# Norm steps fed tile by tile and a pinned matmul order between the dense blocks of a 1024-wide network

## The chip, the cores and the metric

The kernel runs on one core of a Trainium2 chip. The metric is the device time of one execution in microseconds, the median of several executions. The core has five engines that each run their own instruction queue in order: PE (matrix multiply), DVE and POOL (element-wise), ACT (functions, scaled copies) and SP, which issues the loads and stores.

## The reference

The program is two blocks on 512 tokens of width 1024, all in fp32. The first block has two layers: a mixer, a layer norm, a convolutional feed-forward network (FFN), a second layer norm, and an embedding gate. The second block has two hybrid layers with an RMS norm ahead of each, and a final RMS norm. What matters here:

```
for i in range(DEPTH):                                     # 2
    y = mixer_ab(x, ...) if i % 2 == 0 else mixer_c(x, ...)
    x = layer_norm(ALPHA * x + y, ln_mix_g[i], ln_mix_b[i])
    f = conv_ffn(x, ...)                                   # 1024 -> 2816 -> 1024
    x = layer_norm(ALPHA * x + f, ln_ffn_g[i], ln_ffn_b[i])
    x = x + sigmoid(x @ ple_w_gate[i]) * (p[i] @ ple_w_proj[i])
for l in range(DEPTH):
    x = hybrid_layer(x, norm_g[l], w_in[l], ...)           # begins with rmsnorm(x, norm_g)
return rmsnorm(x, final_norm_g)
```

## The kernel before

Activations lie feature-major: `s.x` is eight tiles of 128 features x 512 tokens. Every fp32 matmul is done as three in a reduced fp32 format, from a high and a low part of both operands: `mm3` (lines 351 to 353). The parts come from `split`: ACT rounds to the high part (L400), DVE subtracts to get the low part (L401). Weights arrive as 512 KB units by SP's queue and are split the same way (L326 on ACT, L327 on DVE). PSUM banks have tags: `d` (three), `S` (two), `o` (one), `m` (two); in the profile a tile's name is its tag, and `s` is an SBUF slot of one tile, `sm` a small one.

`project` writes the last dense layer of a block into the residual in two halves of 256 tokens, eight output tiles each, each tile 12 matmuls where the contraction has four operand pairs; `resid` (L981, DVE) adds the tile to `s.x`. When the eight tiles of a half have been emitted, it calls the norm for that half.

A norm of one half is a chain over all engines. For a layer norm: POOL adds the eight tiles up to two (L413), PE takes the mean (L515, tag `m` for half 0, `o` for half 1), DVE subtracts it (L519), ACT squares (L460, L463), DVE (L465) and POOL (L413) add the squares into two tiles, PE sums them over the partitions (L440), DVE adds epsilon (L443), POOL takes the power -1/2 (L431), PE broadcasts the result to all partitions (L448), and DVE and ACT scale and split (L526, L527, L529, L530) into `s.xs`, the operand pairs of the next dense block. The RMS norms lack the mean; their scaling is L486, L492 and L493.

The next dense block is `group`, tiles of 24 matmuls (eight operand pairs), again one half of the tokens after the other: in the FFN two gate and two up tiles at a time, in `ple` four tiles of the embedding gate. `ple` also computes the embedding projections `pp`: eight tiles of six 512-column matmuls from the input `p`, all between the FFN's layer norm and the gate. Before each hybrid layer the four token tiles of V are computed by `dense_v`, 400 columns, one weight unit after the other.

The code emits instructions in program order, and a scheduler then sets the order on each engine. It fills a wait that it foresees with matmuls of tiles further on, if their banks are free. Only the places with `manual_schedule` keep the written order.

Of the kernel before, what the change touches and what calls it, by code (L numbers as in the profile page):

```python
# [20 lines left out]
T = 512  # L21
# [16 lines left out]
# the order of the steps of the mixers  # L38
# [7 lines left out]
v v v v q0 q1 q0 x0 g f0 c x1 x1 q1 x0 x1 x0 c f0 f0 p1 p0 b2 b2 r0 r1 p1 p0 b2 k b1 b2 f1 f1 b2 f1 b1 n0 b2  # L46
# [19 lines left out]


def _cols(v):
    """[n * 128] -> [128, n]"""
    return np.asarray(v).reshape(-1, 128).T  # L70
# [7 lines left out]
def _consts():  # L78
# [11 lines left out]
    # the compressed keys: 31, and one that stands for "no key yet"  # L90
# [7 lines left out]
    # rope: frequencies, phases, and the rows that the angle tables are made of  # L98
# [34 lines left out]
    # compressed hidden row n: rows n of the first half and n + 1 of the second, and the positions' rows 32 and 33  # L133
# [17 lines left out]
def _layout(i):  # L151
    """The arrays that the program reads: what came in, cut and ordered; and constants of the shapes."""
# [7 lines left out]
    # cq, ckv, four copies of the shared rope key, then q and k of each pair of heads  # L160
# [20 lines left out]
    for l in range(2):  # L181
# [21 lines left out]
        # compression: rows (position, feature), two positions to 128 rows; beside each the position 16 later  # L203
# [45 lines left out]
# ---------------------------------------------------------------- program  # L249
class Prog:  # L250
    NSLOT = 74

    def __init__(s, ctx, tc, aps, names):
# [14 lines left out]
        s.ahead = {}  # L268

    # -- memory  # L270
# [12 lines left out]
    def park(s):  # L283
        """s.x goes to DRAM until it is needed again"""
# [34 lines left out]
    # -- weights  # L319
# [10 lines left out]
    def wt(s, name, j, kt, idx=None):  # L330
        """The kt weight tiles of output tile j: [(h, l)]."""
# [14 lines left out]
    def mm3(s, ps, st, mv, first=True, last=True):  # L346
        """ps (+)= sum over k of st[k]^T mv[k], both as (h, l)."""
# [12 lines left out]
    def dense_v(s, name, sv, n, out, tags="dddS"):  # L360
        """token-major, in steps: out = [tokens, n] for the four token tiles"""
# [17 lines left out]

    def run(s, order, steps):  # L380
        """Each word of the order takes the next step of the generator of that name."""
        for w in order.split():
            next(steps[w])
        for w, g in steps.items():
            assert next(g, None) is None, w

    def group(s, specs, mv, tags, evac=None):
        """A few output tiles, one half of the tokens after the other."""
        banks = [s.bank(t) for t, _ in zip(tags, specs)]
        W = [s.wt(n, j, len(mv)) for n, j in specs]  # L390
        for c in HALVES:
            for i, ps in enumerate(banks):
                s.mm3(ps[:, c], W[i], [(h[:, c], l[:, c]) for h, l in mv])
                if evac is not None:
                    evac(i, ps, c)
        return banks

# [6 lines left out]
    # -- sums over features  # L404
# [13 lines left out]
    def colsum(s, ps, t, w):  # L418
        """ps[:, q] = sum over partitions of t[:, 128 q:] * w"""
# [3 lines left out]
    def bcast(s, ps, r, m=128, e=0):  # L423
        """ps[e:e+m, q] = r[q] on every partition"""
# [8 lines left out]
    def rstd(s, ts, w, eps, c=slice(0, 512), tag="m"):  # L433
        """1 / sqrt(eps + the sum over ts and partitions, times w), on every partition"""
# [9 lines left out]
        s.pow_(r[:, :n], r[:, :n])  # L444
        pb = s.bank(tag)
# [6 lines left out]
    def sumsq(s, get, n, c):  # L452
        """two tiles whose sum is the sum of squares of get(j)[:, c]"""
        nc = s.nc
        acc = [s.slot(), s.slot()]
        for j in range(n):
            x = get(j)
            e = j % 2
            if j < 2:
                nc.scalar.activation(acc[e][:, c], x[:, c], AF.Square)  # L460
                continue
            q = s.slot()
            nc.scalar.activation(q[:, c], x[:, c], AF.Square)  # L463
            if e:
                nc.vector.tensor_add(acc[e][:, c], acc[e][:, c], q[:, c])  # L465
            else:
                s.pool_add(acc[e][:, c], acc[e][:, c], q[:, c])
            s.free(q)
        return acc

    def rms(s, tiles, gname, w, evac=None):
        """Takes (0 or 1, half of the tokens): tiles / rms(tiles) * g, as (h, l) in s.out; or handed to evac(j, y, columns)"""
        nc = s.nc
        out = None
        if evac is None:
            out = s.out = []

        def half(i, c):
            if evac is None and not out:
                out.extend((s.slot(F32R), s.slot(F32R)) for _ in tiles)  # L480
            acc = s.sumsq(lambda j: tiles[j], len(tiles), c)
            pb = s.rstd(acc, w, RMS_EPS, c, "mo"[i])
            s.free(*acc)
            for j, x in enumerate(tiles):
                y = s.slot()
                nc.vector.scalar_tensor_tensor(y[:, c], x[:, c], s.col(gname, j), pb[:, c], op0=ALU.mult,  # L486
                                               op1=ALU.mult)
                if evac is not None:
                    evac(j, y, c)
                else:  # L490
                    h, l = out[j]
# [4 lines left out]
        return half  # L496

    def layernorm(s, g, b):
        """Takes (0 or 1, half of the tokens): s.x, in place; and s.xs"""
        nc = s.nc  # L500
        X = s.x

        def half(i, c):
            if i == 0:
                s.xs = [(s.slot(F32R), s.slot(F32R)) for _ in X]
            tag = "mo"[i]
            t0, t1 = s.slot(), s.slot()
            s.pool_add(t0[:, c], X[0][:, c], X[1][:, c])
            s.pool_add(t1[:, c], X[4][:, c], X[5][:, c])
            for j in (2, 3):  # L510
                s.pool_add(t0[:, c], t0[:, c], X[j][:, c])
            s.pool_add(t1[:, c], t1[:, c], X[6][:, c])
            pm = s.bank(tag)
            for k, t in enumerate((t0, t1, X[7])):
# [3 lines left out]
            def cent(j):  # L518
                nc.vector.tensor_sub(X[j][:, c], X[j][:, c], pm[:, c])  # L519
                return X[j]  # L520

            acc = s.sumsq(cent, 8, c)
            pb = s.rstd(acc, s.meanw[:, :1], LN_EPS, c, tag)
            s.free(*acc)
            for j in range(8):
                nc.vector.tensor_mul(X[j][:, c], X[j][:, c], pb[:, c])  # L526
                nc.scalar.activation(X[j][:, c], X[j][:, c], AF.Identity, bias=s.col(b, j), scale=s.col(g, j))  # L527
                h, l = s.xs[j]
                nc.scalar.activation(h[:, c], X[j][:, c], AF.Copy)  # L529
                nc.vector.tensor_sub(l[:, c], X[j][:, c], h[:, c])  # L530

        return half
# [6 lines left out]
    # -- attention  # L539
# [1060 lines left out]
```

## Time and profile before

| | before |
|---|---|
| time, median of 3 | 2556.72 us (2556.55 to 2565.89) |
| span of the profiled execution, first to last instruction | 2549.7 us |
| instructions | 31474 |
| PE busy | 2480.1 us, 97% |
| DVE busy | 1500.2 us, 59% |
| ACT busy | 1014.7 us, 40% |
| POOL busy | 549.6 us, 22% |

The profiled execution's own time outside of the profiler isn't recorded; its span stands beside the median, and the 7.0 us between them lie before the first or after the last instruction. The engines work at once, so their busy times overlap. PE's share says that the kernel's time is PE's work and the few waits in between; which waits those are is read from the stretches in which PE is not busy. N1 to N7 name, in the order of the program, the seven stretches where a norm stands between two dense blocks.

### The profile page before, as it was taken

Reading aid. Unit: us, or ns where it says so; the run is one execution under the profiler, and the core shown is the slowest. Engines: PE = TensorE matmul, PEld = TensorE weight load, DVE = VectorE, ACT = ScalarE, POOL = GpSimd, SP = SyncE. Lnnn points to the kernel's source line nnn. Section 1 sums busy time; section 2 is a strip of 40 time slices with the busy share of each in tenths; the row PEclk is TensorE's granted clock in tenths of the full one; section 3 lists DMA queues with packets and bytes.
Section 4 is the critical chain, followed back from the end, with each engine's and each line's share of the span. In section 5 each row is a group of like instructions: output and inputs, shape, how many; then the busy total and the mean of one; then the engine's idle time right before and its main releaser. Section 6 shows DMA issues by size and latency. Waiting matters only on the chain.

```text
span 2549.7 us, 31474 instructions
## 1 busy us (share of the span) xinstructions
PE 2480.1 (97%) x12224; PEld 1966.5 (77%) x12224; DVE 1500.2 (59%) x2501; ACT 1014.7 (40%) x1606; POOL 549.6 (22%) x529
## 2 busy tenths in 40 slices
PE   9989999999999999999999999999999999999998
PEld 6655688888887676888888888776778887767787
DVE  5698675453655768674453655565553556665434
ACT  5554463242454444353342544433323344333232
POOL 1333321010223534321010330311122103011221
PEclk9999999999999999999999999999999999999999
DMA  5112133232232112133232243221233432212332
GB/s 171 50 42 60 42 99 104 93 98 94 77 128 87 50 38 62 50 100 107 91 101 90 75 145 117 76 67 50 83 105 108 147 100 75 75 42 85 110 95 67
DMA packets 72652, 220.30 MB, mean 86 GB/s; under 512 B 9461, under 2 KB 13558, under 8 KB 72503
## 3 DMA queue, kind: packets, MB, share of 16 engines
q1 hardware_dynamic: 72502, 218.30, 26.6%
q8 instruction: 96, 1.57, 0.3%
q14 instruction: 54, 0.43, 0.1%
HBM read 209.87 MB, written 8.39 MB: 86 GB/s over the span
## 4 chain that ended last, share of the span: by engine, by line
PE 77%; DVE 8%; POOL 4%; ACT 3%; issue 2%; POOLq 0%; DVEq 0%; ACTq 0%
PE d L353 20%; PE d L351 20%; PE d L352 20%; POOL s L413 2%; PE S L647 2%; PE o L623 2%; PE S L571 2%; PE S L351 1%; PE S L352 1%; PE S L353 1%; PE m L426 1%; POOL s L416 1%; DVE l L327 1%; PE m L623 1%; PE o L1062 1%
## 5 line engine op out<-in xcount | busy, mean ns | idle before, releaser
L351 PE MATMUL d<-s,h 128*128 128x512 f32 (+1 forms) x2768 | 1053.1, 381 | 7.0 <-ACT h L326 5.8
L353 PE MATMUL d<-s,l 128*128 128x512 f32 (+1 forms) x2768 | 1050.3, 379 | 1.4 <-DVE l L327 1.4
L352 PE MATMUL d<-s,h 128*128 128x512 f32 (+1 forms) x2768 | 1050.7, 380 | 0.2 <-DVE s L401 0.2
L327 DVE TENSOR_TENSOR l<-st,h 128x1024 fp32r<-128x1024 f32 (+5 forms) x375 | 460.8, 1232 | 483.5 <-ACT h L326 481.6
L326 ACT ACTIVATE h<-st 128x1024 fp32r<-128x1024 f32 (+5 forms) x375 | 387.6, 1035 | 770.3 <-PE d L352 656.0
L351 PEld LDWEIGHTS d<-s,h 128*128 128x128 f32 x2768 | 522.9, 189 | 111.6 <-issue 9.9
L353 PEld LDWEIGHTS d<-s,l 128*128 128x128 f32 x2768 | 523.2, 189 | 105.6 <-issue 9.2
L352 PEld LDWEIGHTS d<-s,h 128*128 128x128 f32 x2768 | 523.4, 189 | 101.3 <-issue 7.9
L413 POOL TENSOR_TENSOR s<-s,s 128x512 f32<-128x512 f32 (+2 forms) x238 | 278.7, 1176 | 671.0 <-DVE s L1390 347.5
L416 POOL TENSOR_TENSOR s<-s,s 128x512 f32<-128x512 f32 (+2 forms) x83 | 125.5, 1512 | 153.6 <-DVE s L544 123.1
L1130 POOL TENSOR_SCALAR s<-s 128x512 f32<-128x512 f32 x44 | 28.8, 655 | 575.6 <-ACT s L1129 575.6
L400 ACT ACTIVATE s<-s 128x512 fp32r<-128x512 f32 (+1 forms) x104 | 65.5, 631 | 172.0 <-DVE s L1134 75.7
L401 DVE TENSOR_TENSOR s<-s,s 128x512 fp32r<-128x512 f32 (+1 forms) x104 | 77.3, 748 | 52.9 <-ACT s L400 52.6
L571 PE MATMUL S<-s,s 128*128 128x512 f32 (+9 forms) x256 | 94.6, 393 | 10.4 <-DVE mt L574 3.6
L638 POOL TENSOR_TENSOR s<-s,s 128x384 f32<-128x384 f32 (+1 forms) x40 | 46.7, 1183 | 260.2 <-PE o L623 255.6
L351 PE MATMUL S<-s,h 128*128 128x256 f32 x352 | 100.8, 287 | 0.1
L352 PE MATMUL S<-s,h 128*128 128x256 f32 x352 | 100.4, 285 | 0.0
L647 PE MATMUL S<-s,s 128*128 128x512 f32 (+6 forms) x368 | 98.4, 379 | 2.0 <-ACT s L651 1.8
L353 PE MATMUL S<-s,l 128*128 128x256 f32 x352 | 99.7, 283 | 0.0
L647 PEld LDWEIGHTS S<-s,s 128*128 128x128 f32 (+3 forms) x368 | 59.1, 187 | 51.1 <-ACT s L651 22.7
L981 DVE TENSOR_TENSOR s<-d,s 128x256 f32<-128x256 f32 (+1 forms) x80 | 41.8, 526 | 84.6 <-PE d L353 84.1
L651 ACT ACTIVATE s<-S 128x512 f32<-128x512 f32 (+4 forms) x136 | 65.9, 518 | 45.8 <-PE S L647 41.2
(254 smaller groups left out, 2670.1 us busy)
## 6 DMA issues: line engine op xcount, KB each, us to landing
st<-in_win SPq DMA_DIRECT2D x112, 512.0 KB, 3.4
st<-in_gu SPq DMA_DIRECT2D x88, 512.0 KB, 3.4
st<-in_dn SPq DMA_DIRECT2D x32, 576.0 KB, 3.6
st<-in_pg SPq DMA_DIRECT2D x16, 512.0 KB, 3.5
st<-in_cqk SPq DMA_DIRECT2D x16, 512.0 KB, 3.4
st<-in_wbr SPq DMA_DIRECT2D x16, 512.0 KB, 3.5
st<-in_wo SPq DMA_DIRECT2D x16, 512.0 KB, 3.5
st<-in_abin SPq DMA_DIRECT2D x14, 512.0 KB, 3.3
```

Of the source, the lines that this page charges most:

```text
L326: s.nc.scalar.activation(h, st, AF.Copy)
L327: s.nc.vector.tensor_sub(l, st, h)
L351: s.nc.tensor.matmul(ps, lhsT=sh, rhs=mh, start=first and k == 0, stop=False)
L352: s.nc.tensor.matmul(ps, lhsT=sh, rhs=ml, start=False, stop=False)
L353: s.nc.tensor.matmul(ps, lhsT=sl, rhs=mh, start=False, stop=last and k == n - 1)
L401: s.nc.vector.tensor_sub(l[:n], x[:n], h[:n])
L413: s.nc.gpsimd.tensor_tensor(o, x, y, op=ALU.add)
L416: s.nc.gpsimd.tensor_tensor(o, x, y, op=ALU.mult)
L571: nc.tensor.matmul(ps[:, :w], lhsT=lq[:, 128 * q:128 * q + 128], rhs=rk[:, :w], start=True, stop=True)
L623: s.nc.tensor.matmul(ps[64 * e:64 * e + 64, o:], lhsT=lhs(e), rhs=rhs[e][:, o:], start=start, stop=stop)
L647: nc.tensor.matmul(ps[:m, o:], lhsT=a[:, 128 * k:128 * k + m], rhs=b[:, o:], start=t == 0, stop=t == len(terms) - 1)
L651: nc.scalar.activation(p[:m, o:], ps[:m, o:], AF.Exp, scale=scale)
```

## The change

The norms become objects with two methods. `feed` is called by `project` (or by the gate's evacuation) for each finished tile and emits its sum or its square at once. `half` is a generator of the remaining chain; it stops after the head, after the mean and the squares, and after the column sum and power, and goes on when `tick` has been called a number of times. `tick` is called after each tile of `project` and `group` (twice per tile in `group`), of the embedding projections, and each contraction step of `dense_vh`. `settle` runs what is left of a norm before its half is read.

Around the tiles of `project`, `group`, `dense_vh` and `pp` stands `manual_schedule` for PE: what is emitted inside keeps its written order on PE, the norm's matmuls among it.

The embedding projections are split: tiles 0 to 3 ahead of the FFN's first group, tiles 4 to 7 where all eight were; the input `p` is loaded and split at the start of the FFN and kept. `dense_vh` computes V in two pairs of token tiles, so that the first pair needs only half 0 of the norm. The parking of the residual in DRAM moves behind V. In the gate's evacuation the residual add of tiles 6 and 7 moves from POOL to DVE. The numbers of matmuls, activations and loads stay the same. The line numbers of the changed kernel differ: 351 to 353 become 352 to 354, 400 and 401 become 456 and 457, 440 becomes 496, 448 becomes 505, 515 becomes 604, 530 becomes 618, 962 to 966 become 1046 to 1050, 981 becomes 1065.

```
     def project(s, name, mv, first, then=None):
...
         for i, c in enumerate(HALVES):
-            for j in range(8):
-                ps = s.bank("dS"[j % 2])
-                s.mm3(ps[:, c], W[j], [(h[:, c], l[:, c]) for h, l in mv])
-                s.resid(j, ps, first, c)
-            then(i, c)
+            with s.tc.manual_schedule(engines={mybir.EngineType.PE}):
+                for j in range(8):
+                    ps = s.bank("dS"[j % 2])
+                    s.mm3(ps[:, c], W[j], [(h[:, c], l[:, c]) for h, l in mv])
+                    s.resid(j, ps, first, c)
+                    then.feed(i, c, j)
+                    s.tick()
+            s.begin(i, then.half(i, c))
...
     def group(s, specs, mv, tags, evac=None):
...
+        n = len(mv)
+        for i, c in enumerate(HALVES):
+            wide = n - 2 if i in s.norms else 0
+            s.settle(i)
+            with s.tc.manual_schedule(engines={mybir.EngineType.PE}):
+                for k in range(wide):
+                    for w, ps in zip(W, banks):
+                        s.mm3(ps[:, c], w[k:k + 1], [(mv[k][0][:, c], mv[k][1][:, c])], k == 0, False)
+                    s.tick()
+                for e, ps in enumerate(banks):
+                    s.mm3(ps[:, c], W[e][wide:], [(h[:, c], l[:, c]) for h, l in mv[wide:]], wide == 0)
+                    if evac is not None:
+                        evac(e, ps, c)
+                    s.tick()
+                    if not wide:
+                        s.tick()
...
+    def tick(s):
+        for i in list(s.norms):
+            n = s.norms[i]
+            n[0] -= 1
+            if n[0] <= 0:
+                n[0] = next(n[1], None)
+                if n[0] is None:
+                    del s.norms[i]
+    def begin(s, i, gen):
+        assert i not in s.norms
+        s.norms[i] = [next(gen), gen]
+    def settle(s, i):
+        if i in s.norms:
+            for _ in s.norms.pop(i)[1]:
+                pass
...
     class Layernorm:
+        def half(n, i, c):
+            yield 2
...
+            yield 6
+            pb = yield from s.rstd(acc, s.meanw[:, :1], LN_EPS, c, tag, 2)
...
     def ffn(s, l):
+        s.ple_in(l)
+        s.ple_proj(l, range(4))
...
     def ple_proj(s, l, js):
+        for j in js:
+            with s.tc.manual_schedule(engines={mybir.EngineType.PE}):
+                ps = s.dense(f"pp{l}", j, s.pt)
+                s.tick()
...
     def ple(s, l):
+        s.ple_proj(l, range(4, 8))
...
-            s.pool_add(s.x[j][:, c], s.x[j][:, c], th[:, c])
+            if j < 6:
+                s.pool_add(s.x[j][:, c], s.x[j][:, c], th[:, c])
+            else:
+                nc.vector.tensor_add(s.x[j][:, c], s.x[j][:, c], th[:, c])
```

Three places show what the pinned order does. The first is PE behind FFN 0, where half 0 of `project` begins. The operand pair numbered 5293 and 5294 (before) or 5371 and 5372 (after) is the last of four; `d` and `S` are output tiles, and three matmuls make one contraction step. Before:

```order
L351 MATMUL S_5363<-s_781_5216,h_5305 128x256
L352 MATMUL S_5363<-s_782_5217,h_5305 128x256
L351 MATMUL d_5321<-s_789_5293,h_5299 128x256
L351 MATMUL S_5335<-s_789_5293,h_5299 128x256
L351 MATMUL d_5349<-s_789_5293,h_5305 128x256
L353 MATMUL S_5363<-s_781_5216,l_5306 128x256
L351 MATMUL S_5363<-s_789_5293,h_5305 128x256
```

After:

```order
L352 MATMUL d_5401<-s_796_5294,h_5377 128x256
L353 MATMUL d_5401<-s_797_5295,h_5377 128x256
L354 MATMUL d_5401<-s_796_5294,l_5378 128x256
L352 MATMUL d_5401<-s_804_5371,h_5377 128x256
L353 MATMUL d_5401<-s_805_5372,h_5377 128x256
L354 MATMUL d_5401<-s_804_5371,l_5378 128x256
L352 MATMUL S_5416<-s_780_5140,h_5377 128x256
```

Before, 35 matmuls on the first three pairs, of four tiles, stand ahead of the first one on the last pair; after the change nine do, those of the first tile.

The second place is PE in the norm behind mixer AB, half 0, after the change: the column sum (L496), the first two of the embedding tiles, the broadcast (L505), the mean of half 1 (L604), two more embedding tiles of six matmuls, and the first FFN tile, `d_2976`. Before, ten matmuls of 256 columns stood between the first pass of the column sum and the broadcast.

```order
L496 MATMUL m_2832<-meanw,s_554_2717 128x1
L352 MATMUL d_2855<-s_571_2843,h_2858 128x512
...
L354 MATMUL d_2873<-s_574_2849,l_2859 128x512
L505 MATMUL m_2880<-identr,sm_2837 128x128 x2
L604 MATMUL o_2915<-s_534_2677,meanw 128x256
...
L354 MATMUL d_2966<-s_574_2849,l_2859 128x512
L352 MATMUL d_2976<-s_536_2693,h_2982 128x256
L353 MATMUL d_2976<-s_537_2694,h_2982 128x256
```

The norm's matmuls moved behind the whole second half of `project`, and twelve 512-column matmuls came between sum and broadcast.

The third is PE where that first FFN group changes from half 0 to half 1. Before, tiles `d_2947` and `S_2948` of half 1 are mixed:

```order
L353 MATMUL d_2947<-s_537_2657,l_2954 128x256
L351 MATMUL S_2948<-s_531_2651,h_2959 128x256
L352 MATMUL S_2948<-s_532_2652,h_2959 128x256
L351 MATMUL d_2947<-s_539_2659,h_2953 128x256
L353 MATMUL S_2948<-s_531_2651,l_2960 128x256
L351 MATMUL S_2948<-s_533_2653,h_2959 128x256
```

After, the last pair of the first tile of half 1 (2706, 2707) stands 24 matmuls of `S_2979` and 21 of its own behind the broadcast:

```order
L505 MATMUL o_3086<-identr,sm_3059 128x128 x2
L352 MATMUL S_2979<-s_536_2693,h_3000 128x256
...
L354 MATMUL S_2979<-s_550_2707,l_3001 128x256
L352 MATMUL d_2976<-s_536_2693,h_2982 128x256
L353 MATMUL d_2976<-s_537_2694,h_2982 128x256
...
L354 MATMUL d_2976<-s_550_2707,l_2983 128x256
L352 MATMUL S_2977<-s_536_2693,h_2988 128x256
```

The mixing is gone: one tile runs through all eight pairs before the next begins.

## Rows read from the trace of the kernel before

**Rows 1.** Page, part 1: busy time, share of the span, instructions by engine.

```profile
PE 2480.1 (97%) x12224; PEld 1966.5 (77%) x12224; DVE 1500.2 (59%) x2501; ACT 1014.7 (40%) x1606; POOL 549.6 (22%) x529
```

**Rows 2.** Table by stretch, N1 to N6: length; engines' busy us; PEclk; DMA share; GB/s.

```profile
309.00:339.00 30.00, 27.54 (x207) 26.64 (x206) 23.55 (x56) 16.89 (x38) 10.70 (x13) 0.94 0.21 65
680.00:718.00 38.00, 33.11 (x190) 28.91 (x189) 27.05 (x60) 22.10 (x48) 15.84 (x18) 0.91 0.22 73
1067.00:1098.00 31.00, 27.98 (x221) 26.97 (x220) 25.17 (x58) 17.53 (x40) 11.12 (x14) 1.00 0.21 67
1438.00:1472.00 34.00, 31.56 (x193) 28.13 (x192) 26.38 (x61) 22.16 (x48) 12.16 (x14) 0.95 0.23 77
1502.00:1532.00 30.00, 26.12 (x183) 24.74 (x182) 16.76 (x40) 10.94 (x27) 11.00 (x12) 0.94 0.51 165
2014.00:2040.00 26.00, 24.66 (x181) 23.19 (x180) 18.83 (x48) 10.97 (x26) 5.55 (x7) 1.00 0.42 148
```

**Rows 3.** PE's waits in N2: waiting line, what for; us in total, times, longest.

```profile
PE o L515 <- POOL s L413: 2.3, 1, 2.3
PE m L448 <- POOL sm L431: 1.1, 1, 1.1
...
PE m L440 <- POOL s L413: 0.4, 1, 0.4
```

**Rows 4.** Table by stretch, columns as rows 2, behind that wait in N2 and N3.

```profile
690.60:694.00 3.40, 3.40 (x18) 3.40 (x17) 2.58 (x8) 2.27 (x6) 0.00 (x0) 0.50 0.52 159
...
1077.00:1080.40 3.40, 3.02 (x25) 3.02 (x26) 2.12 (x7) 1.98 (x6) 0.32 (x1) 1.00 0.49 154
```

**Rows 5.** Timeline of PE in N2, N4: start, us, engine, line, out<-in, shapes, count.

```profile
668.27 0.39 PE L353 MATMUL d<-s,l 128*128 128x512 f32 x1
668.49 0.28 PE L351 MATMUL d<-s,h 128*128 128x256 f32 x1
...
669.57 0.28 PE L351 MATMUL S<-s,h 128*128 128x256 f32 x1
...
672.83 0.39 PE L351 MATMUL d<-s,h 128*128 128x256 f32 x1
...
1426.73 0.28 PE L351 MATMUL d<-s,h 128*128 128x256 f32 x1
```

**Rows 6.** Timeline of ACT and DVE in N2, then of DVE in N4.

```profile
672.14 0.63 ACT L400 ACTIVATE s<-s 128x512 fp32r<-128x512 f32 x1 [1.87 <-DVE s L1134]
...
672.14 1.36 DVE L401 TENSOR_TENSOR s<-s,s 128x512 fp32r<-128x512 f32 x2
...
1431.04 1.47 DVE L401 TENSOR_TENSOR s<-s,s 128x512 fp32r<-128x512 f32 x2 [0.70 <-ACT s L400]
```

**Rows 7.** Timeline of PE, ACT and DVE in N1, first tiles of half 0.

```profile
296.34 0.39 PE L351 MATMUL d<-s,h 128*128 128x256 f32 x1
...
300.02 0.63 ACT L400 ACTIVATE s<-s 128x512 fp32r<-128x512 f32 x1 [2.28 <-DVE s L966]
...
300.69 0.69 DVE L401 TENSOR_TENSOR s<-s,s 128x512 fp32r<-128x512 f32 x1 [0.70 <-ACT s L400]
```

**Rows 8.** Timeline of DVE in N3, end of the last head's chain.

```profile
1059.48 0.75 DVE L1078 SCALAR_TENSOR_TENSOR s<-o,sub,s 128x512 f32<-128x512 f32 x1 [2.97 <-ACT s L1076]
1060.93 0.69 DVE L401 TENSOR_TENSOR s<-s,s 128x512 fp32r<-128x512 f32 x1 [0.70 <-ACT s L400]
```

**Rows 9.** Timeline of PE and DVE in N1, scaling of half 1.

```profile
337.24 0.60 PE L448 MATMUL o<-identr,sm 128*128 128x128 f32 x4
...
339.77 0.76 DVE L530 TENSOR_TENSOR s<-s,s 128x256 fp32r<-128x256 f32 x2
...
344.57 0.76 DVE L530 TENSOR_TENSOR s<-s,s 128x256 fp32r<-128x256 f32 x2 [0.84 <-ACT s L529]
```

**Rows 10.** PE's longest wait in N5, columns as rows 3.

```profile
PE o L440 <- POOL s L413: 3.0, 1, 3.0
```

**Rows 11.** Timeline of DVE in N5, the last sum of squares.

```profile
1525.76 0.42 DVE L465 TENSOR_TENSOR s<-s,s 128x256 f32<-128x256 f32 x1 [1.07 <-ACT s L463]
```

More of the change, by code (lines that the diff above doesn't have):

```diff
@@ L268, in __init__ @@
         s.ahead = {}
+        s.norms = {}
     def slot(s, dt=F32):
@@ L378, in dense_v, with dense_vh @@
         yield
+    def dense_vh(s, name, sv, n, out):
+        d = s.a[name]
+        per, nu = d.shape[2], d.shape[0]
+        banks = [s.bank(t) for t in "dddS"]
+        W = []
+        for u in range(nu):
+            h, l = s.unit(d[u], list(d.shape[2:]))
+            W += [(h[:, r], l[:, r]) for r in range(per)]
+        for i in range(2):
+            s.settle(i)
+            with s.tc.manual_schedule(engines={mybir.EngineType.PE}):
+                for k, (h, l) in enumerate(sv):
+                    for q in (2 * i, 2 * i + 1):
+                        c = slice(128 * q, 128 * q + 128)
+                        s.mm3(banks[q][:, :n], [(h[:, c], l[:, c])], W[k:k + 1], k == 0, k == len(sv) - 1)
+                    s.tick()
+            for ps in banks[2 * i:2 * i + 2]:
+                v = s.slot()
+                s.nc.scalar.activation(v[:, :n], ps[:, :n], AF.Copy)
+                out.append(v)
+            yield
     def run(s, order, steps):
@@ L450, in rstd, with square @@
         return pb
-    def sumsq(s, get, n, c):
+    def square(s, acc, j, x, c):
         nc = s.nc
[L455 to L469, printed above, removed]
@@ L471, in rms @@
-    def rms(s, tiles, gname, w, evac=None):
-        nc = s.nc
[L474 to L489, printed above, removed]
+        if j < 2:
+            acc.append(s.slot())
+            nc.scalar.activation(acc[j][:, c], x[:, c], AF.Square)
+            return
@@ new lines, in square, with scaled, rms @@
+        q, e = s.slot(), j % 2
+        nc.scalar.activation(q[:, c], x[:, c], AF.Square)
+        if e:
+            nc.vector.tensor_add(acc[e][:, c], acc[e][:, c], q[:, c])
+        else:
+            s.pool_add(acc[e][:, c], acc[e][:, c], q[:, c])
+        s.free(q)
+    def scaled(s, x, g, pb, c):
+        y = s.slot()
+        s.nc.vector.scalar_tensor_tensor(y[:, c], x[:, c], g, pb[:, c], op0=ALU.mult, op1=ALU.mult)
+        return y
+    def rms(s, tiles, gname, w):
+        nc = s.nc
+        acc, c = [], slice(0, 512)
+        for j, x in enumerate(tiles):
+            s.square(acc, j, x, c)
+        r = s.rstd(acc, w, RMS_EPS)
+        next(r)
+        try:
+            next(r)
+        except StopIteration as e:
+            pb = e.value
+        s.free(*acc)
+        out = []
+        for j, x in enumerate(tiles):
+            y = s.scaled(x, s.col(gname, j), pb, c)
+            out.append(s.split(y))
+            s.free(y)
+        return out
@@ new lines, with __init__, feed @@
+    class Rms:
+        def __init__(n, s, gname, evac=None):
+            n.s, n.gname, n.evac, n.acc = s, gname, evac, {}
+            if evac is None:
+                s.out = []
+        def feed(n, i, c, j):
+            n.s.square(n.acc.setdefault(i, []), j, n.s.x[j], c)
+        def half(n, i, c):
+            s = n.s
+            nc = s.nc
+            yield 2
+            if n.evac is None and not s.out:
+                s.out.extend((s.slot(F32R), s.slot(F32R)) for _ in range(8))
+            pb = yield from s.rstd(n.acc[i], s.meanw[:, :1], RMS_EPS, c, "mo"[i], 2)
+            s.free(*n.acc[i])
+            for j, x in enumerate(s.x):
+                y = s.scaled(x, s.col(n.gname, j), pb, c)
+                if n.evac is not None:
+                    n.evac(j, y, c)
@@ L1151, in ple, with ple_proj @@
             nc.sync.dma_start(t, a["p"][l, k])
-            pt.append(s.split(t))
+            s.pt.append(s.split(t))
             s.free(t)
-        pr = []
-        for j in range(8):
-            ps = s.dense(f"pp{l}", j, pt)
-            t = s.slot()
-            nc.scalar.activation(t, ps, AF.Copy, scale=0.5)
-            pr.append(t)
-        for h, lo in pt:
+    def ple_proj(s, l, js):
+        for j in js:
+            with s.tc.manual_schedule(engines={mybir.EngineType.PE}):
+                ps = s.dense(f"pp{l}", j, s.pt)
+                s.tick()
+            t = s.slot()
+            s.nc.scalar.activation(t, ps, AF.Copy, scale=0.5)
+            s.pr.append(t)
+    def ple(s, l):
+        nc, a = s.nc, s.a
+        s.ple_proj(l, range(4, 8))
+        pr = s.pr
+        for h, lo in s.pt:
             s.free(h, lo)
         s.new = [None] * 8
-        H = s.rms(s.x, "ng0", s.meanw[:, :1]) if l == 1 else None
+        H = s.Rms(s, "ng0") if l == 1 else None
         def evac(j, ps, c):
@@ L1175, in evac @@
             if l == 1 and j == 7:
-                H(HALVES.index(c), c)
+                s.begin(HALVES.index(c), H.half(HALVES.index(c), c))
         s.group([(f"pg{l}", j) for j in range(4)], s.xs, "dSdS", evac)
@@ L1189, in hybrid @@
         H = s.out
-        s.park()
         win = f"win{l}"
@@ L1210, in hybrid, with park @@
         F = []
+        def park():
+            s.park()
+            yield
         def gates():
@@ L1341, in branch @@
                 yield
-        steps = {"v": s.dense_v(f"vin{l}", H, 400, V), "g": gates(), "k": keys(), "c": comp()}
+        steps = {"v": s.dense_vh(f"vin{l}", H, 400, V), "z": park(), "g": gates(), "k": keys(), "c": comp()}
         for j in range(2):
@@ L1365, in hybrid @@
             if c == 1:
-                then = s.rms(s.x, "ng1", s.meanw[:, :1]) if l == 0 else s.final()
+                then = s.Rms(s, "ng1") if l == 0 else s.final()
             s.project(f"wo{l}{c}", A, False, then)
```

89 lines of the change are left out of this document (47 added, 42 removed).

## The prediction

> **What bounds the kernel now.** I read the page first, then the stretches around the norms, then single instructions. PE is busy 97% of the span [rows 1], so a change can gain only where PE waits or runs slowly, and any new PE wait costs its full length. The change moves work only in seven stretches, those where a norm hangs between two dense blocks: N1 behind mixer AB, N2 behind FFN 0, N3 behind mixer C, N4 behind FFN 1, N5 the RMS norm before hybrid 0, N6 the one before hybrid 1, N7 the final one. The table by stretch [rows 2] shows PE idle for 2.5, 4.9, 3.0, 2.4, 3.9 and 1.3 us in N1 to N6.
>
> Idle time understates the loss twice over. The end of a matmul is modelled: 256 columns show 0.28 us, but starts follow every 0.12 us (nine starts from 668.49 to 669.57), and 512 columns every 0.22 to 0.23 [rows 5]; so each gap costs about 0.16 us more than it shows. And PE's clock drops: behind the 1.1 us wait of N2 for POOL's power the granted clock is 0.50 (1.2 instead of 2.4 GHz) for 3.4 us, while N3, whose list has an equal line, stays at 1.00 [rows 3, 4]. Five of these drops lie in the seven stretches: one each in N1, N4 and N5, two in N2. In the 3.4 us 18 matmuls began where the usual spacing gives 28, ten or 1.2 us short; by the distances of the starts, with the slow tail, a drop costs 1.4 us. Counting every stretch by the distance of starts beyond the usual spacing, the losses are N1 5.2, N2 9.6, N3 4.2, N4 5.3, N5 6.5, N6 2.6, N7 0.9 (before the end chain): **34.3 us**, some 7 of it clock. That is the most the change can win.
>
> **What goes.** In N1 to N4 the column sum waits for POOL's sum of squares, the broadcast for POOL's power, and in N2 the second mean for POOL's adds for 2.3 us [rows 3]. After the change the column sum (L496) stands behind the whole second half of `project`, 12 embedding matmuls (12 x 0.227 = 2.7 us) lie between it and the broadcast (L505), and twelve more behind that. The chain between sum and broadcast is 0.16 us (adding epsilon) plus 0.7 to 1.6 us on POOL, so it is hidden. I take all of N1 to N4 as gone: 5.2 + 9.6 + 4.2 + 5.3 = **-24.3 us**. The embedding matmuls, their copies and weights keep their number; they only stand in another place, and the 512 kB loads of their weights go by the same queue. The six residual adds that go from POOL to DVE cost DVE 0.42 us each in N5 and are inside its chain there.
>
> **What comes, first place: the first tile of `project`.** Its last contraction step needs the operand pair that was computed last. Before, the first half of tokens runs 9, 9, 9 and 8 matmuls of four tiles before it touches that pair. Pinned, it runs 9 and then wants the pair at once (first excerpt of the order). In N2 the nine start at 668.49, the next begin at 669.57, and the first matmul on the last pair ran at 672.83 [rows 5]; ACT began the high part at 672.14 (0.63 us), the low part is the second of DVE's two, from 672.82 to 673.50 [rows 6]. The pinned tile therefore ends at 673.50 + 0.12 instead of 668.49 + 1.44: a loss of **3.7 us**, of which 3.2 are one wait. N4 has the same picture: its tile starts at 1426.73 [rows 5], DVE's low part runs from 1431.04 for 0.74 [rows 6], which gives 1431.9 - 1428.2 = **3.7**. In N1 the tile starts at 296.34, ACT's high part at 300.02, DVE's low part ends at 301.38 [rows 7]. There a part of the embedding input's split now stands inside the chain, on ACT between L1046 and L1047 and on DVE before L1048: one more 0.63 to 0.69, so the tile ends at 302.2 instead of 297.8: **4.4**. In N3 the last head's chain ends with DVE 1059.48 + 0.75 and the low part at 1061.62 [rows 8]; its own column sum and broadcast, which had dense matmuls between and behind them, now stand bare (I estimate 1.2 and 1.4 us of waiting, then 2.9 for the pair), less 1.1 us that the place loses already: **4.4**. Sum **+16.2 us**. Nothing covers it: all rows of the block are behind the waiting matmul in PE's fixed order.
>
> **Second place: the first tile behind the norm.** The scaling hands over operands pair by pair. In N1's second half the broadcast starts at 337.24, and DVE finishes pairs of low parts at 340.53 (339.77 + 0.76) and 345.33 (344.57 + 0.76) [rows 9], that is 3.3, 4.9, 6.5 and 8.1 us behind the broadcast, two operands each; DVE waits for ACT between them. Before, PE gets there with 30 matmuls as cover and then runs two tiles mixed, so that nothing is lost. Now one tile of 24 matmuls stands between (0.36 + 24 x 0.12 = 3.2), and the next, alone, cannot end before 8.1 + 0.72 = 8.8 us instead of 3.2 + 2.9 = 6.1: **2.7 us**, in three pieces of at most 0.9. In the first half the cover is the other half's mean (0.9) and two embedding tiles (2.7), 4.0 with the broadcast: 8.8 - 6.9 = **1.9 us**. Four times both: **+18.4 us**. Zero would need 3 us more cover per half; the order shows none.
>
> **The clock.** Rows bound the price from 0 (N3) to 1.4 us per wait. The four waits of 3.2 us and more are longer than any that left the clock alone, so I take four drops, 5.6 us; of the eight broken waits I take two, 2.8 us: **+8.4**. The Trainium skill, page "Perfetto Trace Analysis", section "Matmul Optimizations", says that the matmul engine scales its power by utilization, so matmuls should be issued back to back in batches. By that rule contiguous pinned batches would spare the clock, and the sum would be rival 1's. The trace agrees in that the drops stand behind waits; but the pinned batches here begin with one.
>
> **The rest.** N5 loses 3.0 us to POOL's sums [rows 10] and a drop. Afterwards the two last residual adds are DVE's, but its 16 scaling steps, six multiply-adds and four weight splits stand before the last sum of squares, which was added at 1525.76 [rows 11], 15.3 us behind the first broadcast; the order leaves PE 84 matmuls, 11.3 us, until it needs the sum. I take 4.1 us of waiting with the broadcast pinned right behind, and one drop: 5.5 instead of 6.5, **-1.0**. N6: the first half's waits go (0.9), but the same scaling chain now has to meet pinned V tiles: **0**. N7: the two first-half waits go, **-0.9**; the chain at the end is as before. `park` behind V and `dense_vh` change no count; their loads have a queue that is not busy.
>
> **Sum.** -24.3 + 16.2 + 18.4 + 8.4 - 1.9 = **+16.8 us**. The profiled execution spans 2549.7 us; the median of the three times is 2556.72, 7.0 more, which lies outside the span and stays. 2549.7 + 16.8 + 7.0 = **2573.5 us**.
>
> **Rivals.** (1) *Waits trade one for one.* The drops do not come with the new waits, as in N3: -24.3 + 34.6 - 1.9 - 1.4 (N5's drop) = +7.0, **2564 us**. For it speaks N3, and that the waits behind the norms are broken; against it, that three stretches of four with a 1.1 us wait dropped. (2) *The operands come sooner.* ACT and DVE have less beside them while PE stands still, the pairs follow every 1.2 instead of 1.6 us (last at 6.9): the second place costs 1.5 + 0.7 per stretch, 8.8 instead of 18.4; then -24.3 + 16.2 + 8.8 - 1.9 = -1.2, and four drops bring +4.4: **2554 to 2561 us**. Against it: the pace was 1.6 us in N1's second half, where DVE stood idle 0.84 us before the last pair [rows 9]. (3) *The change does what it says*: the norm's waits go and the pinned order finds its operands ready. Then -24.3 - 1.9 = -26, **2530 us**. The one mechanism that could do it is that everything upstream, the last operand pair and the scaling, arrives 3 to 4 us earlier relative to PE; the point where it turns to a gain is when first and second place together cost less than 26 us, against my 34.6. Against it stand the stamps of rows 5 to 9. (4) *All waits drop the clock*: twelve drops, 16.8 instead of 8.4: **2582 us**.
>
> **How the numbers follow.** Forecast with some drops, or all: 0.60. Rival 1: 0.22; rival 2: 0.11; rival 3: 0.07. A difference below 0.5% (12.8 us) can hardly be measured on this kernel. Faster than 2543.9: rival 3 and a part of the uncertainty in the sums, 0.10. Slower than 2569.5: 0.58. Between: 0.32. The range reaches from rival 2 to beyond rival 4, **2551 to 2588 us**; below it lies rival 3 alone.
>
> **What would show it.** Right: in the first tile of N1 to N4's `project`, PE waits 3 to 4 us for ACT's and DVE's splits (L456, L457); in the first tile behind each norm, some 2 us for DVE's L618; L496 and L505 wait for nothing in N1 to N4; more stretches than before at a granted clock of 0.50. Wrong: PE idle in N1 to N4 below 13 us in all, or first tiles that run through. The step I trust least is the clock, then the cover of the first tile behind the norm.

## The result and the profile after

The changed kernel takes 2578.3 us (median of 4, 2577.17 to 2582.66) against 2557.15 us for the kernel before on the same chip: 1.0073 times as long, with a 95% interval of 1.0057 to 1.0089, that is 15 to 23 us slower. The forecast was slower by 16.8 us, 2573.5 us, with a range of 2551 to 2588 us.

The page, part 1, first row: busy time, share of the span and instructions of each engine. Behind it the first group of part 5, whose last part is PE's idle time just before these matmuls and what ended it.

```profile
PE 2497.2 (97%) x12224; PEld 1976.4 (77%) x12224; DVE 1508.9 (59%) x2507; ACT 1014.0 (39%) x1606; POOL 552.1 (21%) x523
...
L352 PE MATMUL d<-s,h 128*128 128x512 f32 (+1 forms) x2768 | 1057.2, 382 | 23.5 <-ACT s L456 13.1
```

PE's count is that of [rows 1], its busy time is 17 us longer: it does the same work, more of it at a lower clock (mean granted clock 0.988, before 0.994). And the first matmul of a contraction step now waits for ACT's split (L456) for 13.1 us. Before, the same wait (there L351 for L400) cost 1.0 us. PE's lists of waits say what PE waited for, us in total, times, longest; first the line of the kernel before, then those of the changed kernel:

```profile
PE d L351 <- ACT s L400: 1.0, 1, 1.0
```

```profile
PE d L352 <- ACT s L456: 13.1, 6, 3.5
...
PE d L352 <- ACT s L617: 4.5, 15, 0.8
...
PE o L496 <- POOL s L469: 3.8, 3, 2.4
...
PE o L496 <- DVE s L519: 3.2, 3, 1.8
...
PE m L505 <- POOL sm L487: 1.3, 5, 0.3
```

L456 is the first place of the prediction, L617 (ACT's high parts behind a norm) the second. POOL's power, 1.1 us in each layer norm before [rows 3], costs PE 0.3 us now.

To see where the time went I compared the starts of equally numbered matmuls in the two traces, at marks outside of the stretches N1 to N7 where both orders are the same. The table gives by how much each stretch of a trace is longer than in the profiled execution of the kernel before; the column "rest" is everything else. This table is worked out from the traces' starts; it is not a view of the profile.

| us against before | N1 | N2 | N3 | N4 | N5 | N6 | N7 | N1 to N7 | rest |
|---|---|---|---|---|---|---|---|---|---|
| forecast | +5.9 | +0.8 | +6.9 | +5.1 | -1.0 | 0 | -0.9 | +16.8 | 0 |
| changed kernel | +4.8 | +0.5 | +6.8 | +6.2 | +2.9 | +1.1 | -0.8 | +21.4 | +5.8 |
| project not pinned | -1.0 | -4.7 | +0.5 | +1.0 | +3.0 | +1.1 | -0.8 | -0.9 | +6.1 |
| group not pinned | +2.4 | -1.9 | +4.5 | +2.6 | +2.8 | +1.1 | -1.0 | +10.4 | +5.9 |
| project and group not pinned | -3.3 | -7.0 | -1.9 | -2.3 | +4.0 | -0.4 | -0.6 | -11.6 | +12.7 |
| old V | +4.7 | +0.5 | +8.2 | +6.1 | -0.3 | -0.3 | -1.0 | +17.8 | +2.1 |
| project, group not pinned, old V | -3.3 | -7.0 | -1.9 | -2.3 | +2.5 | -0.3 | -1.0 | -13.3 | +5.6 |
| two tiles mixed, pinned | +2.4 | -1.6 | +5.9 | +2.5 | +3.7 | +1.1 | -1.0 | +13.0 | +8.7 |
| no split of the projections | +2.9 | -7.1 | +5.4 | -2.2 | 0.0 | -0.3 | -1.0 | -2.3 | +5.7 |

(N1 to N4 of a row hold the whole of that norm, its `project` and the group behind it.) The forecast's row is what the sum of the prediction gives for each stretch.

"Rest" is not the change: its instructions and their order are the same, and nearly all of it lies before 290 us and between 740 and 1040 us, inside the mixers (with both pins undone 2.4 us more lie at a drop in hybrid 0). Each trace is one execution, and the clock drops there differ from one to the next. So the whole spans, 2549.7 and 2577.0 us, overstate the change by some 6 us, and the ratio of the times is the better measure of the whole; the columns N1 to N7 say where.

### The profile page after: what moved, and what is told of

The parts are those of the page before. It is cut to its first block, busy times and chain, and to the rows that moved or that the text cites. A ratio compares the mean times of both kernels' runs of the same rounds, so it can differ in the third digit from the quotient of the medians.

```text
span 2577.0 us, 31482 instructions
## 1 busy us (share of the span) xinstructions
PE 2497.2 (97%) x12224; PEld 1976.4 (77%) x12224; DVE 1508.9 (59%) x2507; ACT 1014.0 (39%) x1606; POOL 552.1 (21%) x523
## 4 chain that ended last, share of the span: by engine, by line
PE 76%; DVE 7%; ACT 5%; POOL 4%; issue 2%; POOLq 0%; DVEq 0%; ACTq 0%
PE d L353 20%; PE d L354 20%; PE d L352 20%; POOL s L469 2%; PE o L709 2%; PE S L733 2%; PE S L657 2%; PE S L353 1%; PE S L352 1%; PE S L354 1%; PE m L482 1%; ACT s L615 1%; POOL s L472 1%; PE m L709 1%; PE o L1149 1%
## 5 line engine op out<-in xcount | busy, mean ns | idle before, releaser
L352 PE MATMUL d<-s,h 128*128 128x512 f32 (+1 forms) x2768 | 1057.2, 382 | 23.5 <-ACT s L456 13.1
L469 POOL TENSOR_TENSOR s<-s,s 128x512 f32<-128x512 f32 (+2 forms) x232 | 277.0, 1201 | 679.4 <-DVE s L1499 347.5
L456 ACT ACTIVATE s<-s 128x512 fp32r<-128x512 f32 (+1 forms) x109 | 68.7, 631 | 175.2 <-DVE s L1223 77.3
L657 PE MATMUL S<-s,s 128*128 128x512 f32 (+9 forms) x256 | 94.3, 392 | 10.4 <-DVE mt L660 3.6
```

What stands on the lines that cost most here:

```text
L352: s.nc.tensor.matmul(ps, lhsT=sh, rhs=mh, start=first and k == 0, stop=False)
L456: s.nc.scalar.activation(h[:n], x[:n], AF.Copy)
L469: s.nc.gpsimd.tensor_tensor(o, x, y, op=ALU.add)
L657: nc.tensor.matmul(ps[:, :w], lhsT=lq[:, 128 * q:128 * q + 128], rhs=rk[:, :w], start=True, stop=True)
```

## The new waits in the trace

In N1, the first tile of `project` after the change: PE's last matmul that was ready, the first on the last operand pair, ACT's and DVE's splits around them.

```profile
300.19 0.28 PE L354 MATMUL d<-s,l 128*128 128x256 f32 x1
303.96 0.38 PE L352 MATMUL d<-s,h 128*128 128x256 f32 x1 [3.48 <-ACT s L456]
```

```profile
299.28 0.60 ACT L1046 ACTIVATE s<-m 128x512 f32<-128x512 f32 x1 [0.22 <-PE m L709]
299.77 0.62 ACT L456 ACTIVATE s<-s 128x512 fp32r<-128x512 f32 x1
300.29 0.62 ACT L1047 ACTIVATE s<-s 128x512 f32<-128x512 f32 x1
303.28 0.63 ACT L456 ACTIVATE s<-s 128x512 fp32r<-128x512 f32 x1 [2.37 <-DVE s L1050]
```

PE stands from 300.3 to 303.96, since the pair's high part leaves ACT at 303.9, as [rows 7] led to expect. The split of the embedding input stands between L1046 and L1047 (299.77) and delays that chain by 0.5 us. N2 has the same picture against [rows 5]:

```profile
682.45 0.28 PE L354 MATMUL d<-s,l 128*128 128x256 f32 x1
685.83 0.39 PE L352 MATMUL d<-s,h 128*128 128x256 f32 x1 [3.10 <-ACT s L456]
```

By the distance of the starts, the first tile loses 4.5 us in N1, 4.0 in N2 and 4.2 in N4. In N3 the bare column sum (L477), the broadcast (L482) and the first tile begin 1.0, 1.9 and 2.5 us late, 5.4 together. PE's list of waits there, 1055 to 1130 us:

```profile
PE d L352 <- ACT s L456: 2.1, 1, 2.1
PE m L482 <- POOL sm L487: 1.7, 1, 1.7
...
PE m L477 <- ACT s L1153: 0.7, 1, 0.7
```

In all four places the clock drops, in N1, N2 and N4 behind the wait, in N3 already behind the broadcast's, so that the wait of the first tile lies inside the drop. The table by stretch: window, its length, busy time (and count) of PE, PEld, DVE, ACT, POOL, then PEclk, the granted clock, DMA share and GB/s.

```profile
304.90:308.30 3.40, 3.40 (x18) 3.40 (x18) 0.85 (x2) 0.00 (x0) 0.00 (x0) 0.51 0.00 0
687.20:690.60 3.40, 3.40 (x18) 3.40 (x18) 0.75 (x2) 0.00 (x0) 0.70 (x1) 0.51 0.02 5
1069.50:1076.30 6.80, 4.52 (x21) 3.93 (x20) 1.90 (x4) 1.23 (x2) 0.00 (x0) 0.50 0.10 39
1455.20:1458.60 3.40, 3.40 (x18) 3.40 (x18) 0.84 (x2) 0.00 (x0) 0.00 (x0) 0.51 0.00 0
1547.30:1557.50 10.20, 6.89 (x24) 6.68 (x25) 6.85 (x19) 3.23 (x8) 1.09 (x2) 0.51 0.61 203
```

As in [rows 4], 18 matmuls begin in N1, N2 and N4 where 28 would. The fifth row is N5; it is three times as long as any drop in a norm before, but in 3.3 us of it PE shows no work.

Behind the norm of N1's half 1, PE and DVE after the change:

```profile
348.80 0.60 PE L505 MATMUL o<-identr,sm 128*128 128x128 f32 x4
...
354.55 0.38 PE L352 MATMUL d<-s,h 128*128 128x256 f32 x1 [0.21 <-ACT s L617]
...
356.15 0.39 PE L352 MATMUL d<-s,h 128*128 128x256 f32 x1 [0.28 <-ACT s L617]
```

```profile
351.33 0.76 DVE L618 TENSOR_TENSOR s<-s,s 128x256 fp32r<-128x256 f32 x2
353.00 0.75 DVE L618 TENSOR_TENSOR s<-s,s 128x256 fp32r<-128x256 f32 x2
354.53 0.76 DVE L618 TENSOR_TENSOR s<-s,s 128x256 fp32r<-128x256 f32 x2 [0.77 <-ACT s L617]
356.13 0.76 DVE L618 TENSOR_TENSOR s<-s,s 128x256 fp32r<-128x256 f32 x2 [0.84 <-ACT s L617]
```

The pairs come every 1.6 us, the last 8.1 us behind the broadcast, exactly the pace of [rows 9]. PE's first matmul on each of the last two pairs begins when DVE has started that pair's low part. The shown idle times, 0.21 and 0.28, look small because of the modelled ends; by the distance of the starts this tile loses 2.3 us, that of half 0 loses 1.2. No clock drop follows.

## Experiments

All are the changed kernel with the edit shown; ratios are against the kernel before, run beside them.

### Undo one pin, or both

```
# project                                     # group
-            with s.tc.manual_schedule(...):
+            with ExitStack():
```

`project` alone:

> The changed kernel with one edit: the order of PE is not pinned in project. First theory (the first tile waits): the waits of some 4 us and the clock drops behind them at N1 to N4 go, about 18 us of waiting and 5 of clock, so some 20 us below the changed kernel, 2556 to 2560 us. Rival (the pinning only shows a lateness that has another cause, the split of the embedding input or the earlier feeding): the scheduler finds nothing to fill in, and the time stays at 2574 to 2580 us.

2556.94 us, ratio 0.9992 (0.9983 to 1.0001), 0.8% below the changed kernel's ratio. By stretch N1 to N4 are 5.7, 5.2, 6.3 and 5.2 us shorter, 22.4 in all. PE's waits in N1 (290 to 360 us) hold no L456 any more, and the granted clock at the place of the first drop is back at 1.00:

```profile
PE d L352 <- ACT s L617: 0.8, 3, 0.3
PE m L505 <- POOL sm L487: 0.3, 1, 0.3
```

```profile
304.00:307.40 3.40, 3.40 (x31) 3.40 (x30) 1.55 (x5) 0.00 (x0) 2.83 (x4) 1.00 0.02 5
```

So the pin makes the wait, and the drop comes and goes with the wait: neither the feeding nor the split makes them. This one line of the change costs as much as the whole change does.

`group` alone:

> The changed kernel with one edit: the order of PE is not pinned in group. First theory (second place): two tiles mix behind each norm, and of the 3.9 us per layer norm (1.2 in half 0, 2.7 in half 1) more than half goes: 8 to 14 us below the changed kernel, 2564 to 2570 us. Rival (the scaling itself is late because the embedding tiles and the other half's steps stand in front of it): under 4 us, 2574 us or more.

2571.27 us, ratio 1.0046 (1.0034 to 1.0058). N1 to N4 are 2.4, 2.4, 2.3 and 3.6 us shorter, 10.7 in all, within what was expected; the median's gain is 7 us, so that it ends 1.3 us above the expected 2564 to 2570. L617 no longer stands in PE's list of N1; the sum of squares (L469) does, with 0.7 us. That is a new wait: mixed, the tiles reach the column sum of half 1 before POOL's sum is there.

Both:

> Both edits: neither project nor group is pinned. First theory: the two gains add, some 30 us below the changed kernel and 8 to 14 below the kernel before, 2543 to 2550 us, since the waits that the change removed stay away. Rival (the removed waits come back with the scheduler's own order): the time of the kernel before, 2555 to 2560 us.

2549.44 us, ratio 0.9962 (0.9949 to 0.9975), faster than the kernel before. The gains add (32.7 us over N1 to N4, against 22.4 + 10.7), and the removed waits stay away: POOL's power costs 0.3 us in N1, not 1.1.

### Pin another order

Is it pinning that costs, or the order that is pinned? In `project`, half 0, four tiles run over all pairs but the last, then each takes the last pair; still pinned:

```
+    w = len(mv) - 1 if i == 0 else 0
+    B = [s.bank("dS"[j % 2]) for j in range(4)] if w else []
+    for j, ps in enumerate(B):
+        s.mm3(ps[:, c], W[j][:w], [(h[:, c], l[:, c]) for h, l in mv[:w]], True, False)
...
+        s.mm3(ps[:, c], W[j][k:], [(h[:, c], l[:, c]) for h, l in mv[k:]], k == 0)
```

> The changed kernel, project still pinned, but written in another order: in half 0 the first four tiles run over all operand pairs but the last, then each takes the last pair. First theory (what costs is the order that is pinned, not pinning): as much as without the pin, 2555 to 2560 us. Rival (a fixed order costs by itself, since the scheduler cannot move the norm's matmuls around it): 2565 us or more.

2561.95 us, ratio 1.001 (0.9999 to 1.0021): 16 us of the 20 that the free order gains, a little short of the expectation, and not the rival's 2565. It is the order, mostly. In the traces N3 is 3.0 us longer than with the free order, where the last head's column sum and broadcast stay bare.

The same idea for the group behind each norm, four tiles by operand pairs:

> As the run before, and in the first group behind each layer norm the four tiles take one operand pair after the other (12 matmuls or 1.44 us for each pair, against a pair of low parts every 1.6 us per two tiles), pinned. First theory: the waits behind the norms go too, 12 to 16 us below the run before, 2540 to 2546 us. Rival (four tiles at once need four weight units early, and PE waits for their splitting instead): 2550 us or more.

2599.34 us, ratio 1.0159 (1.0145 to 1.0174): the rival's side, and worse than it said, but for another reason. PE, then ACT, in N1:

```profile
334.56 0.28 PE L353 MATMUL S<-s,h 128*128 128x256 f32 x1
...
339.98 0.49 PE L353 MATMUL d<-s,h 128*128 128x256 f32 x1 [4.90 <-ACT s L1259]
```

```profile
336.60 0.70 ACT L620 ACTIVATE s<-s 128x256 fp32r<-128x256 f32 x2
337.21 0.70 ACT L517 ACTIVATE s<-s 128x256 f32<-128x256 f32 x2
337.83 1.62 ACT L520 ACTIVATE s<-s 128x256 f32<-128x256 f32 x5
339.36 0.57 ACT L1259 ACTIVATE s<-d 128x512 f32<-128x512 f32 x1
```

The third tile needs a `d` bank at once. That bank still holds an embedding projection, and its copy (L1259) stands in ACT's queue behind the whole scaling and the squares of the other half. PE waits 4.9 us, and a clock drop of 6.8 us follows. Tile by tile this bank is wanted 42 matmuls, 5.0 us, later. The same wait stands in N2, N3 and N4 (19.6 us in the four), and two more of 4.4 us for the evacuation of the gate's own tiles (L1273). With the old V beside it nothing changes:

> Both dense blocks pinned in the order by pairs, and V computed as before. If all three losses are separate, 2.6 us below the run with both in the order by pairs: 2538 to 2543 us, the fastest. Rival as there: 2548 us or more.

2598.28 us, ratio 1.0156 (1.014 to 1.0171).

Only the first two tiles mixed, whose banks are free:

```
+    if s.fresh and e < 2:
+        if e == 0:
+            for k, (h, l) in enumerate(mv):
+                for w, p in zip(W[:2], banks):
+                    s.mm3(p[:, c], w[k:k + 1], [(h[:, c], l[:, c])], k == 0, k == n - 1)
```

> The changed kernel, everything still pinned, but the first two tiles of the first group behind each layer norm take one operand pair after the other in turn (12 matmuls, 1.44 us, for two pairs of low parts that come every 1.6 us). Theory (second place, and the banks of four tiles were what failed before): PE is at the first pair 3.2 us behind the broadcast and needs 5.8 us for both tiles, which gives 9.0 us against operands that are complete at 8.1 and used up by 9.5, so of 3.9 us per norm some 0.5 stays: 10 to 14 us below the changed kernel, 2563 to 2568 us. Rival (the wait only moves to the next tile or to the splitting of the second weight unit): 2572 us or more.

2575.89 us, ratio 1.0059 (1.0046 to 1.0072), the rival's number. By stretch N1 to N4 are 2.3, 2.1, 0.9 and 3.6 us shorter, 8.9 together, about what the free group gives, and the tiles of N1's half 1 now lose 0.2 us by the starts instead of 2.3. (`fresh` marks the first group behind a norm.) N5 and "rest" are 3.7 us longer in that execution, and N3 has a longer drop in its first tile. By the ratios the gain is 3.6 us, and their intervals reach 3 and 4 us to either side; so that the mixing removes the waits of its place is shown by the trace, and how much of it the time keeps is not settled.

### V, and what is left of the pins

The V tiles as before the change, not pinned, `park` ahead of them:

```
-        steps = {"v": s.dense_vh(f"vin{l}", H, 400, V), "z": park(), ...
+        steps = {"v": s.dense_v(f"vin{l}", H, 400, V), ...
```

> The changed kernel with V computed as before (four token tiles by weight unit, not pinned, both halves of the norm finished first) and the residual parked ahead of it. If the pinned V pairs are what made N5 and N6 3.0 and 1.3 us longer than in the kernel before, 3 to 5 us below the changed kernel, 2573 to 2575 us. Rival (N5 is late because of DVE, whose queue now holds the last adds in front of the sum): no change, 2577 to 2580 us, or slower.

2575.26 us, ratio 1.0064 (1.0052 to 1.0076): between the expectation and the rival, and inside the interval of the changed kernel's 1.0073, so the times don't settle it. In the traces N5 is 3.2 and N6 1.4 us shorter; both are back at the kernel before. The changed kernel's waits in N5, and those with the old V:

```profile
PE o L496 <- POOL s L469: 2.4, 1, 2.4
PE o L496 <- DVE s L519: 1.8, 1, 1.8
PE o L505 <- POOL sm L487: 1.0, 1, 1.0
```

```profile
PE o L496 <- POOL s L469: 2.4, 1, 2.4
PE o L505 <- POOL sm L487: 1.2, 1, 1.2
```

POOL's sum is late in both. Pinned, the column sum's four passes stand in a row, so PE waits for the second sum (DVE's, 1.8) too, where the free order puts V matmuls between the passes. The second wait, 1.8 to 2.0 us, stands so in the changed kernel and in the runs with one pin or both undone, where V is still in pinned pairs, and not in this run. The edit takes back the pairs, their pin and the place of `park` together; no run separates the three.

The rest of the difference in N5 goes with the drop, and that isn't V's alone. It is 3.4 us long here and 10.2 with the pinned pairs. But three runs below have the old V with `project` and `group` free, and the same order on PE in N5 as this run; N5 is 2.5 us longer than before in the first, 2.3 in the second (no pin at all, not in the table) and as long as before in the third (no split). In the first two PE waits 0.6 us more, for POOL's first sum, and has more slow clock; the first has a drop as long as the pinned pairs':

```profile
1515.60:1525.80 10.20, 9.57 (x32) 8.99 (x33) 4.80 (x15) 2.49 (x5) 1.51 (x1) 0.51 0.62 214
```

N6 is alike: its 1.1 us come with a drop of 3.4 us at 2062.8 us, and with both pins undone, V still pinned, N6 has neither.

Old V with `project` and `group` free:

> Neither project nor group pinned, and V computed as before. The gain of the old V, 2.6 us in the changed kernel, should add: 2545 to 2548 us, 0.4 to 0.5% below the kernel before. Rival (the old V's gain depends on the pinned gate group in front of it): 2549 us or more.

2543.68 us, ratio 0.9942 (0.9927 to 0.9957), a little below the expected 2545. This beats both kernels: 15 us below the one before. With nothing pinned at all, not the embedding projections either:

> Nothing is pinned (project, group, embedding projections) and V is computed as before; the feeding by tiles, the steps and the split embedding projections stay. If the gain over the kernel before comes from the places at which the steps are emitted, 2541 to 2547 us as with the embedding projections pinned. Rival (without any pin the scheduler puts the column sums back between the tiles of project, where they waited): 2550 us or more.

2546.26 us, ratio 0.9942 (0.9928 to 0.9956), the same. And with the two mixed tiles pinned in a free rest:

> Project not pinned, the two mixed tiles pinned as in the run before, V computed as before. If pinned and free mixing are worth the same, the time of the version with project and group free and the old V, 2541 to 2546 us. Rival (the free group gains because it also moves other tiles): 2548 us or more.

2545.86 us, ratio 0.9944 (0.9931 to 0.9956), the same again. So none of the pins brings anything that these runs can tell (their intervals reach some 0.0014 to either side). The gain comes from what all three keep: the emission in steps, the split projections and the adds moved to DVE. Of these only the split was tested by itself.

The split itself, undone in the free version with the old V:

```
-        s.ple_in(l)
-        s.ple_proj(l, range(4))
...
-        s.ple_proj(l, range(4, 8))
+        s.ple_in(l)
+        s.ple_proj(l, range(8))
```

> Project and group not pinned, V as before, and all eight embedding projections in their old place behind the FFN's norm: N1 and N3 lose the 24 matmuls of 512 columns, 5.4 us, that stand around their first broadcast, N2 and N4 have 5.4 us more. If those are what hides the norm's chain, N1 and N3 lose 3 to 5 us each: 2550 to 2554 us. Rival (the scheduler finds other cover, as in the kernel before): under 2548 us.

2553.96 us, ratio 0.9977 (0.9967 to 0.9987): 9 us of the 15 are gone, more than half. N1 and N3 are 6.2 and 7.2 us longer than with the split, 1.2 and 2.2 us above the expected 3 to 5: without the cover PE waits twice for ACT's high parts (L617, 1.9 us each in N1) and the clock drops again, once in N1 and twice in N3; N2 and N4 stay as they are, so eight tiles there hide no more than four. N5 is 2.5 us shorter in this execution, with the same order: its drop is 3.4 us long instead of 10.2.

## Why the prediction was right, and where it was off

**What goes.** Nearly as said. The waits for POOL's power went from 1.1 to 0.3 us per norm. But 0.2 us stays at the mean, 0.5 at the broadcast and 0.2 behind it, some 0.9 us per norm that I counted as gone: 3.6 us too much gain.

**First place.** Right in mechanism, place and size. I took 3.7, 3.7, 4.4 and 4.4 us for N2, N4, N1 and N3 with one drop of 1.4 each, 21.8 in all; undoing the pin of `project` gave back 22.4. The waits for L456 were 3.1 to 3.5 us in N1, N2 and N4; in N3 it was 2.1, because the broadcast's 1.7 us came ahead of it.

**Second place.** Right in mechanism. The pace of the pairs is the one read before. The size was 1.2 instead of 1.9 us in half 0, and 2.3 in N1 and N3, 2.6 in N2, 4.2 in N4 with the tile ahead instead of 2.7 in half 1: 16.2 instead of 18.4 in all. Undoing the pin of `group` gave back 10.7 of it, since the column sum of half 1 then comes 0.8 to 1.3 us too early in each norm. In half 0 the cover was longer: the first tile began 4.6 us behind the broadcast (0.55 for itself, 1.1 for the mean, 3.0 for the two tiles) instead of 4.0, and ended after 8.7 us, where I had 8.8.

**The clock.** Four drops in the four places with long waits, as taken, the one in N3 6.8 us long instead of 3.4; none behind the eight broken waits, where I had taken two (2.8 us too much). That the waits bring these drops, and not pinned batches as such, is shown by the run with `project` free, which has none of the four while `group` is still pinned. The sentence of the Trainium skill (page "Perfetto Trace Analysis", section "Matmul Optimizations"), that matmuls should run back to back in batches, agrees with these traces in that the order that keeps PE fed is the free one (granted clock 1.00 at the first place), while the pinned batches begin with a wait (0.51 behind it). Pinning did not spare the clock.

**N5 and N6.** Here the step was wrong, and its sign too: -1.0 and 0 were +2.9 and +1.1. I estimated 4.1 us of waiting with one drop; by the starts it was about 7 us of waiting, because the pinned passes wait for both sums one after the other, and the drop was three times as long, though 3.3 us of it lie inside the waits. I had also written that `dense_vh` costs nothing because it changes no count. The wait for the second sum stands only where V is in pinned pairs; what else of N5 and N6 belongs to V, and not to drops that differ from one execution to the next, stays open.

**The span.** "7.0 us outside the span" was wrong. In the changed kernel's profiled execution the time exceeds the span by 1.8 us (2578.77 and 2577.0). The profiled execution of the kernel before was simply some 5 us faster than the timed ones; the forecast's end, which was set on the median, does not depend on it.

The errors partly cancel: 3.6 us too much gain, 2.2 and 2.8 too much cost, 5.0 too little in N5 and N6. That the sum came out within 5 us of the measured time is in part luck; that N1 to N4 cost 18 us more, in the two places named, is not. All four rivals fell, though by the time alone rival 4 (2582 us) is as near as the forecast; the trace tells them apart. Rival 1 (no drops) would have needed the clock at 1.00 behind the first tiles, where the trace has 0.51; rival 2 would have needed the pairs every 1.2 us, where they came every 1.6; rival 3 would have needed operands that are ready; rival 4 would have needed drops behind the broken waits.

## What to carry to other kernels

Fixing an engine's order fixes its waits too: before pinning a block, ask for each operand of its first tile when it is ready, and put what arrives last at the end of several tiles, not of one. Independent work placed where a chain hangs (here half of the embedding projections, 9 us) pays without any pin; but see which bank or slot that work holds and where in another engine's queue its release stands. When a long wait is followed by a slow clock, its price is the wait plus the drop.

## What was not expected

The length of a drop. In N1 to N5 of the kernel before every drop lasted 3.4 us; behind the waits of N5 it lasted 10.2 us in the changed kernel and in five of the twelve experiments. And the mixers, whose order is the same in all versions, have drops that come in one execution and not in another. Inside mixer C the kernel before and the version with `project` free:

```profile
1008.00:1011.40 3.40, 3.40 (x13) 3.02 (x13) 0.41 (x3) 1.19 (x2) 1.26 (x1) 0.50 0.00 0
```

```profile
1002.90:1013.10 10.20, 10.07 (x36) 9.04 (x37) 3.52 (x9) 3.15 (x6) 2.78 (x2) 0.51 0.00 0
```

The same order on PE runs at half clock for 3.4 us in one and 10.2 in the other. This is where the 2 to 13 us of "rest" in the table come from for the most part, and why single spans can't be compared to better than that here. What decides the length of a drop stays open; no run was made for it.
